# Bidirectional encoder in fp32: a doubled weight operand in DRAM, narrower reloads and a new instruction order

## The chip, the core and the metric

The kernel runs on one core of a Trainium2 chip, in one launch. A core has five instruction queues: TensorE (PE in the profile; the loading of its stationary operand is PEld), VectorE (DVE), ScalarE (ACT), GpSimd (POOL) and SyncE (SP). Data moves between DRAM and on-chip memory through 16 DMA engines, which are fed by SyncE's queue (q1 in the profile) and GpSimd's queue (q0). The metric is device time in microseconds (us), the median over the runs of one kernel; lower is better. The notebook-style names in the profile's rows, such as `wlo<-wraw,whi`, say which tile an instruction wrote and which it read.

## What is computed

Two layers (DEPTH = 2) over 256 tokens of width 4096, in fp32. Each layer is, cut from the reference:

```python
h = rmsnorm(x, norm_w[l])
proj = h @ w_in[l]                                   # 4096 x 11264
aq, ak, av, ag, rq, rk, rv, rg = jnp.split(proj, SPLIT_POINTS, axis=-1)
...
a_out = (jax.nn.silu(ag) * gqa_attention(aq, ak, av)).astype(x.dtype)
...
r = bidirectional_retention(rq, rk, rv, log_gf, log_gb).transpose(0, 2, 1, 3)
r = rmsnorm(r, ret_norm[l]).reshape(B, S, RET_WIDTH)
r_out = (jax.nn.silu(rg.astype(jnp.float32)) * r).astype(x.dtype)

x = x + jnp.concatenate([a_out, r_out], axis=-1) @ w_out[l]      # 4096 x 4096
```

Queries and keys of both branches go through an axial rotary embedding (those of attention through an RMSNorm per head as well); attention has 16 query heads over 4 key/value heads, retention 8 heads with a decay forward and one backward. A last RMSNorm follows the second layer. The two big products, `w_in` and `w_out` of each layer, are nearly all of the work.

## The kernel before, in words

**Stages and blocks.** There are four stages: the `w_in` product of layer 1 (11 blocks), its `w_out` product (4 blocks), and the same two for layer 2. A block makes 1024 columns of output for all 256 tokens, as two column halves of 512. It runs over all 4096 input features in 16 pairs of 128-feature slices (pair p holds slices 2p and 2p+1). The weights of one block and pair are a 256 x 1024 matrix, stored in DRAM as two pages of 128 partitions x 2 x 512 numbers (512 KB each).

**High and low parts.** TensorE multiplies fp32r numbers, which carry fewer bits than fp32. So each page is split: ScalarE casts it to a high part (`whi`, or `bhi` for a half page), VectorE subtracts that from the page and gets the low part (`wlo`, `blo`). The operand from x is split in the same way (`x8h`/`x8l`, `x7h`/`x7l`). One product is then three matmuls of 128 x 512: high by high, high by low, low by high (lines 1669 and 1679).

**Eights and sevens.** With two slices, two column halves and two token halves a pair needs 8 products, so 24 matmuls (tiles with an 8 in their name). For six of the 16 pairs (SEVENS) a Strassen-like scheme needs only 7 products, so 21 matmuls. That scheme takes sums of weight quarters. Page A of such a pair holds two diagonal quarters. The DRAM layout holds the other two as the "third" and one that is added to both halves of page A: ScalarE copies page A (`wraw`) to `wv`, and an accumulating DMA on GpSimd's queue (line 723) adds the off-diagonal quarter to both halves of `wv`, read from DRAM as a broadcast, twice the same 2 KB per partition. VectorE then makes two more sums, `wu`, from page A, `wv` and the third. So a product of a seven needs a chain: load of `wraw`, copy on ScalarE, DMA with add, cast on ScalarE, subtraction on VectorE. Its operands of x (`x7h`, `x7l`) need sums too (`xf`, in `split_pair`).

**What sets the order.** The program is written out by Python code that keeps a clock of its own (`Now`, `Clock`) and decides, matmul by matmul, what the other engines are told to do next: `tick` runs after every product, `Weights.proceed`, `low_parts`, `add_up` and `add` issue casts, subtractions, copies and adds, and `Weights.room` says whether there is room for a step of the other tasks. Such tasks are generators: rotary and transposes, attention, retention, residual and norms, and the making of the next stage's operands (`split_pair`). Every engine executes its own list in order. The constants of the planner (STEP_V, EARLY, LOW_AHEAD and so on) can differ by block: `assume(n)` loads BASE and the entry n of PLANS, with blocks counted from 0 to 29 over all stages. LATE goes into the gate of the attention tasks through `near(LATE)`.

**Order of the pairs.** In the first block of a stage the order of the pairs is that of `opening_order`: the eights in rising order, with the sevens inserted at the places of SPREAD (stage 1), SPREAD1, SPREAD2 and SPREAD3. A seven opens a group, and the pages of the eights in its group are put between its own pages.

**Buffers.** Raw pages (`wraw`) have 6 buffers, high parts 5 (RING), low parts 4 (LOWS), `wv` 2, `wu` 1. `Weights.empty` marks a raw page as read; the next load (line 523, SyncE) is told to go when the oldest page still held has been read, so pages are freed in order. A seven's page A is held until its sums `wu` are made.

**Handing on between stages.** Results of a block are turned (32 x 32 transposes on VectorE, `turned`), stored to DRAM by GpSimd (`store`, four DMAs) and fetched again as `full` pages by the next stage (line 916). The last two pages of a stage are not stored: ScalarE moves them on chip (`move`, tiles `ca` and `cb`), scales them by the norm's gains (`nw`) and splits them. Keys and values of attention lie in `kv_dram` as one page of four parts per group: high and low parts of the keys, high and low parts of the values. `attention_scores` uses the keys, `attention_rest` the values, and each fetches the whole page (lines 1315 and 1338). `retention_weights` fetches rk and rq of two heads with runs of 64 numbers (line 1352).

The functions that the diff touches follow.

Of the kernel before, what the change touches and what calls it, by code (L numbers as in the profile page):

```python
# [17 lines left out]
P = 128  # L18
# [9 lines left out]
NB = 512  # L28
# [3 lines left out]
MT = SEQ // P  # L32
NP = KT // 2
BLK = 32
ALL = slice(None)
PAGES = 13
RAWS = 6
SUMS = 2
# [5 lines left out]
STRICT = 4  # L44
RELIEF = 1.5
# [9 lines left out]
V_FIXED = 0.1  # L55
STT = 0.0
# [45 lines left out]
LATE = 25  # L102
# [9 lines left out]
    3: {'U_SLACK': 0.3, 'HOLD': 2, 'LOW_AHEAD': 1.0, 'STRICT': 4},  # L112
    7: {'V_FIXED': 0.14, 'RUSH': 1.0, 'ADD_SLACK': 0.3},
    8: {'SUM_SLACK': 1.0, 'ADD_SLACK': 0.3, 'TIGHT_A': 4, 'LOW_AHEAD': 5.0},
    17: {'EARLY': 1.8, 'V_FIXED': 0.14},
    22: {'TIGHT_B': 20, 'PASS': 0.1, 'STT': 0.0, 'RAW_SLACK': 3.0},
    23: {'RELIEF': 1.5, 'LOW_AHEAD': 5.0},
    24: {'LOW_AHEAD': 5.0},
    25: {'STRICT': 9, 'RUSH': 1.0},
# [216 lines left out]
def hybrid_encoder(  # L336
# [5 lines left out]
    w_out: bass.AP,  # L342
    norm_wT: bass.AP,
# [127 lines left out]
    class Seven:  # L471

        def __init__(self, w):
            self.third, self.added = w[1, :, 1, :], w[1, :, 0:1, :].to_broadcast([P, 2, NB])
            self.a = self.b = self.v = self.u = None
            self.a_at = self.b_at = self.v_at = self.u_at = 0.0

    class Weights:


        def __init__(self):
            self.pages, self.sevens = [], []
            for l in range(DEPTH):
                for w, n in ((w_in, N_IN), (w_out, N_OUT2)):
                    for b in range(n):
                        stage = 2 * l + (w is w_out)
                        start = (l, b) == (0, 0) and w is w_in
                        for g in GROUPS[stage] if b else FIRST_GROUPS[stage]:
                            for slot in slots_of(g, stage, start):
# [10 lines left out]
                                if one.seven:  # L500
                                    if one.kind == PAGE_A:
                                        self.sevens.append(Seven(w[l, b, one.pair]))
                                    one.own = self.sevens[-1]
# [6 lines left out]
            self.raws = [g for g in self.seq if not g.seven or g.kind == PAGE_A]  # L510
            self.placed, self.emptied, self.made = 0, 0, 0
# [655 lines left out]
    def rotary(v, L, kind, to):  # L1167
# [37 lines left out]
        turned(o, v)  # L1205
# [141 lines left out]
    def retention_weights(L, i):  # L1347

        raw = page([P, 2, 4 * MT, 2 * BLK], "rkq")
        for k in range(2):  # L1350
            src = rkq_dram[i // 2][k].rearrange("p (k n) -> p k n", k=4 * MT)
            nc.gpsimd.dma_start(raw[:, k], src[:, :, 2 * BLK * (i % 2) : 2 * BLK * (i % 2 + 1)])
# [3 lines left out]
        v = raw.rearrange("p k (a m) (i t) -> p k m i a t", m=MT, t=BLK)  # L1356
# [596 lines left out]
    for _ in range(RAWS + 1 - 2 * len(NATIVE)):  # L1953
        weights.load()
# [69 lines left out]
    "x", "xT", "w_in", "w_out", "norm_wT", "q_norm", "k_norm", "decay", "final_norm", "consts",  # L2024
# [45 lines left out]
```

## Time and profile before

| | |
|---|---|
| median of 3 runs | 2610.96 us (2609.42 to 2612.77) |
| profiled execution, device time | 2609.15 us |
| its span, first to last instruction | 2607.4 us |
| mean granted TensorE clock | 0.998 |
| DMA | 657.72 MB, mean 252 GB/s |
| queue of SyncE (q1) | 147040 packets, 472.99 MB, 51.5% of 16 engines |
| queue of GpSimd (q0) | 81696 packets, 181.44 MB, 31.4% of 16 engines |
| wraw loads | 776 of 512 KB |
| adds into wv | 180 of 512 KB |

How to read it: the time of a run is that of the profiled execution's kind, its span is 1.75 us shorter. A row of groups gives line, engine, operation, output and inputs, count, then busy us and the mean of one in ns, then idle time before it and what ended that. A row of stretches gives the stretch, its length, then busy us and instructions of PE, PEld, DVE, ACT and POOL, then the granted TensorE clock, the busy share of the DMA engines, and GB/s. A row of waits gives who waited for whom, us in total, times, longest. A timeline row gives start, us, engine, line, operation, tiles, count and, in brackets, idle time before it and its releaser. A row of DMA issues ends with the size in KB and the median us from issue to landing. A matmul of 128 x 512 is shown 0.39 us long while the next starts after 0.23 us, since matmuls overlap. On this kernel a change of under about 5 us can't be told from none.

### The profile page before, as it was taken

To read this page: it belongs to the slowest core of one execution; us is meant where nothing else is said; L and a number is where in the kernel's file an instruction comes from. 1 tells how busy PE (TensorE), PEld (TensorE's weight loads), DVE (VectorE), ACT (ScalarE), POOL (GpSimd) and SP (SyncE) were. 2 spreads that over 40 slices of the span, in tenths; PEclk is the share of its full clock that TensorE was granted. 3 is DMA by queue.
4 is the path that set the end of the run, shared out by engine and by line. 5 is a ranking of instruction groups with operands and counts; after the bars stand their busy time and mean duration, and the time that the engine had idled before them with its cause. 6 is when DMAs were issued, how large, how long until landed. Compare 5 with 4: busy or idle time off the path is not lost.

```text
span 2607.4 us, 34348 instructions
## 1 busy us (share of the span) xinstructions
PE 2585.2 (99%) x11560; PEld 2135.3 (82%) x11560; DVE 2213.8 (85%) x2702; ACT 1848.1 (71%) x2623; POOL 457.8 (18%) x548
## 2 busy tenths in 40 slices
PE   9999999999999999999999999999999999999998
PEld 6888888888888888888787888888888888888886
DVE  6898888888878898777888888889888798987777
ACT  7877776776666778656886667776676667786655
POOL 0112322221112101211112112221211111011110
PEclk9999999999999999999999999999999999999999
DMA  9988988988778777988888889888887797778886
GB/s 307 298 238 285 283 252 260 290 251 267 213 226 254 231 227 223 283 268 250 270 259 243 248 248 286 244 279 270 262 270 211 200 271 234 229 217 257 253 239 194
DMA packets 229634, 657.72 MB, mean 252 GB/s; under 512 B 24784, under 2 KB 31440, under 8 KB 229456
## 3 DMA queue, kind: packets, MB, share of 16 engines
q1 hardware_dynamic: 147040, 472.99, 51.5%
q0 software_dynamic: 81696, 181.44, 31.4%
q8 instruction: 90, 1.47, 0.2%
q10 hardware_dynamic: 720, 1.10, 0.1%
q14 instruction: 88, 0.72, 0.1%
HBM read 611.39 MB, written 44.04 MB: 251 GB/s over the span
## 4 chain that ended last, share of the span: by engine, by line
PE 90%; DMA 4%; DVE 2%; ACT 2%; issue 2%; POOL 0%; SPq 0%; DVEq 0%; POOLq 0%; ACTq 0%
PE M L1669 58%; PE M L1679 29%; PE M L1143 1%; PE M L1144 1%; PE M L1142 1%; DMA pT<-p_dram 1%; DMA wv<-in_w_in 1%; ACT whi L320 1%; DMA wv<-in_w_out 1%; DVE wlo L320 1%; DMA x_dram<-ca 1%; DMA full<-next_dram 0%; DMA wraw<-in_w_in 0%; DVE cb L320 0%; DMA wraw<-in_w_out 0%
## 5 line engine op out<-in xcount | busy, mean ns | idle before, releaser
L320 DVE TENSOR_TENSOR wlo<-wraw,whi 128x1024 fp32r<-128x1024 f32 (+1 forms) x774 | 935.3, 1215 | 159.3 <-issue 60.9
L320 ACT CAST whi<-wraw 128x1024 fp32r<-128x1024 f32 (+1 forms) x776 | 798.1, 1045 | 270.7 <-PE M L1669 259.5
L1669 PE MATMUL M<-whi,x8h 128*128 128x512 f32 x2368 | 923.5, 390 | 3.5 <-ACT x8h L320 2.9
L1669 PE MATMUL M<-whi,x8l 128*128 128x512 f32 x2368 | 922.5, 390 | 0.6 <-DVE x8l L320 0.6
L1679 PE MATMUL M<-wlo,x8h 128*128 128x512 f32 x2364 | 676.7, 389 | 1.4 <-DVE wlo L320 1.4
L1669 PEld LDWEIGHTS M<-whi,x8h 128*128 128x128 f32 x2368 | 445.1, 188 | 97.7 <-ACT x8h L320 3.7
L1669 PEld LDWEIGHTS M<-whi,x8l 128*128 128x128 f32 x2368 | 445.1, 188 | 93.4 <-DVE x8l L320 1.1
L1679 PEld LDWEIGHTS M<-wlo,x8h 128*128 128x128 f32 x2364 | 441.9, 188 | 93.4 <-DVE wlo L320 3.1
L1669 PE MATMUL M<-whi,x7h 128*128 128x512 f32 x1080 | 420.4, 389 | 0.0
L1669 PE MATMUL M<-whi,x7l 128*128 128x512 f32 x1080 | 420.3, 389 | 0.0
L723 POOL DMA_DIRECT2D wv<-in_w_in x132 | 162.2, 1230 | 1040.1 <-ACT wv L320 862.8
L1679 PE MATMUL M<-wlo,x7h 128*128 128x512 f32 x1080 | 334.1, 390 | 1.6 <-DVE wlo L320 1.5
L320 ACT CAST whi<-wv 128x1024 fp32r<-128x1024 f32 x180 | 189.2, 1051 | 133.0 <-DMA wv<-in_w_in 52.3
L320 DVE TENSOR_TENSOR wlo<-wu,whi 128x1024 fp32r<-128x1024 f32 x180 | 219.2, 1218 | 33.6 <-PE M L1679 19.9
L320 DVE TENSOR_TENSOR wlo<-wv,whi 128x1024 fp32r<-128x1024 f32 x180 | 219.5, 1220 | 32.0 <-PE M L1679 27.9
L320 ACT CAST whi<-wu 128x1024 fp32r<-128x1024 f32 x180 | 189.3, 1051 | 79.2 <-DVE wu L320 48.2
L320 ACT COPY wv<-wraw 128x1024 f32<-128x1024 f32 x180 | 188.9, 1049 | 78.9 <-DMA wraw<-in_w_in 39.8
L1679 PEld LDWEIGHTS M<-wlo,x7h 128*128 128x128 f32 x1080 | 202.1, 188 | 45.8 <-DVE wlo L320 4.1
L1669 PEld LDWEIGHTS M<-whi,x7h 128*128 128x128 f32 x1080 | 202.8, 188 | 42.3 <-ACT whi L320 0.3
L1669 PEld LDWEIGHTS M<-whi,x7l 128*128 128x128 f32 x1080 | 202.7, 188 | 41.9
L320 DVE TENSOR_TENSOR wu<-wraw,wv 128x512 f32<-128x512 f32 x180 | 123.4, 686 | 41.1 <-DMA wv<-in_w_in 24.7
L723 POOL DMA_DIRECT2D wv<-in_w_out x48 | 58.1, 1211 | 504.1 <-ACT wv L320 412.3
(249 smaller groups left out, 2381.5 us busy)
## 6 DMA issues: line engine op xcount, KB each, us to landing
wraw<-in_w_in SPq DMA_DIRECT2D x568, 512.0 KB, 5.1
wraw<-in_w_out SPq DMA_DIRECT2D x208, 512.0 KB, 5.1
wv<-in_w_in POOLq DMA_DIRECT2D x132, 512.0 KB, 8.1
third<-in_w_in SPq DMA_DIRECT2D x132, 256.0 KB, 5.6
wv<-in_w_out POOLq DMA_DIRECT2D x48, 512.0 KB, 8.8
third<-in_w_out SPq DMA_DIRECT2D x48, 256.0 KB, 5.3
full<-next_dram POOLq DMA_DIRECT2D x18, 512.0 KB, 9.6
kv<-kv_dram POOLq DMA_DIRECT2D x16, 512.0 KB, 8.6
```

What stands on the lines that cost most here:

```text
L320: return call(out, *args, **kwargs)
L723: self.adds.pop(0)[1]()
L1142: nc.tensor.matmul(out, a[0], b[0], start=start, stop=False)
L1143: nc.tensor.matmul(out, a[0], b[1], start=False, stop=False)
L1144: nc.tensor.matmul(out, a[1], b[0], start=False, stop=stop)
L1669: nc.tensor.matmul(acc[name], a[i], g.hi[h], start=m == first[name] and not i, stop=False)
L1679: nc.tensor.matmul(acc[name], a, g.lo[h], start=False, stop=m == final[name])
```

## The change

- **Doubled quarters.** The host writes for each of the pairs in EVER (the six sevens) the off-diagonal quarter twice side by side into new inputs `twice_in` and `twice_out`. The accumulating DMA into `wv` reads rows of 2 x 512 numbers (4 KB) there, instead of the same 512 numbers (2 KB) twice from the weights. The bytes that the DMA moves stay the same.
- **kv by halves.** `attention_scores` fetches parts 0 and 1 (keys) of the page, `attention_rest` parts 2 and 3 (values).
- **Rows by head.** rk and rq are turned by two transposes (one for each half of the tokens) into a layout in which the two heads that `retention_weights` reads have 128 numbers side by side instead of 64.
- **Free slots.** The six raw buffers are six tiles of their own. A page that is read frees its slot at once, and the next load takes the slot that has been free longest. A loop that would move the first page of sevens ahead by A_EARLY places is added, with A_EARLY = 0.
- **Orders.** LATE goes from 25 to 35. The entries of PLANS are replaced. SPREAD, SPREAD1 and SPREAD3 are changed, SPREAD2 is not.

The diff, without the lines that only pass the new inputs on:

```diff
-LATE = 25
+LATE = 35
...
-    22: {'TIGHT_B': 20, 'PASS': 0.1, 'STT': 0.0, 'RAW_SLACK': 3.0},
...
+    14: {'STRICT': 9, 'TIGHT_A': 0},
+    15: {'S_FIXED': 0.16, 'LONG': 2, 'EARLY': 1.8, 'PASS': 0.3, 'PE_REST': 2.0, 'NEAR': 30},
...
-SPREAD = (4, 5, 7, 10, 12, 14)
-SPREAD1 = (4, 7, 8, 10, 12, 13)
+SPREAD = (3, 5, 8, 11, 12, 13)
+SPREAD1 = (4, 7, 8, 10, 12, 14)
 SPREAD2 = (2, 3, 6, 7, 10, 13)
-SPREAD3 = (4, 7, 8, 9, 10, 13)
+SPREAD3 = (6, 7, 9, 11, 12, 14)
...
-        def __init__(self, w):
-            self.third, self.added = w[1, :, 1, :], w[1, :, 0:1, :].to_broadcast([P, 2, NB])
+        def __init__(self, w, twice):
+            self.third, self.added = w[1, :, 1, :], twice
...
+            for i, g in enumerate(self.raws):
+                if g.seven and i > RAWS + A_EARLY:
+                    self.raws.insert(i - A_EARLY, self.raws.pop(i))
+            self.slots = [f"wraw{_i}" for _i in range(RAWS)]
...
-                g.raw = t(wp, [P, 2, NB], "wraw", RAWS)
+                g.slot = self.slots.pop(0)
+                g.raw = t(wp, [P, 2, NB], g.slot, 1)
...
-            g.empty = True
-            while self.emptied < len(self.raws) and self.raws[self.emptied].empty:
-                self.emptied += 1
-                self.load()
+            self.slots.append(g.slot)
+            self.load()
...
+    def turned_by_head(src, room):
+
+        for m in range(MT):
+            ve.transpose(
+                room.rearrange("p (b i m t) -> p m b i t", b=4, i=4, m=MT)[:, m],
+                src[:, m, :].rearrange("p (i b e) -> p b i e", i=4, e=BLK),
+            )
...
-        turned(o, v)
+        (turned if kind in ("aq", "ak") else turned_by_head)(o, v)
...
-        nc.gpsimd.dma_start(kv, kv_dram[g])
+        nc.gpsimd.dma_start(kv[:, 0:2, :], kv_dram[g][:, 0:2, :])
...
-        nc.gpsimd.dma_start(kv, kv_dram[g])
+        nc.gpsimd.dma_start(kv[:, 2:4, :], kv_dram[g][:, 2:4, :])
...
-        raw = page([P, 2, 4 * MT, 2 * BLK], "rkq")
+        raw = page([P, 2, 4, 2 * MT * BLK], "rkq")
         for k in range(2):
-            src = rkq_dram[i // 2][k].rearrange("p (k n) -> p k n", k=4 * MT)
-            nc.gpsimd.dma_start(raw[:, k], src[:, :, 2 * BLK * (i % 2) : 2 * BLK * (i % 2 + 1)])
+            src = rkq_dram[i // 2][k].rearrange("p (a f) -> p a f", a=4)
+            nc.gpsimd.dma_start(raw[:, k], src[:, :, 2 * MT * BLK * (i % 2) : 2 * MT * BLK * (i % 2 + 1)])
...
+    def twice(o):
+
+        d = np.empty(o.shape[:2] + (len(EVER), P, 2, NB), o.dtype)
+        for i, p in enumerate(EVER):
+            for h in range(2):
+                d[:, :, i, :, h] = o[:, :, p, 1, :, 0]
+        return d
```

Apart from the added transposes and three PSUM copies (`out<-M`) that ScalarE now makes, every engine executes the same instructions as before; the order of TensorE's 11566 rows differs in 289, those of VectorE and ScalarE in about half, mostly by neighbours that have changed places.

More of the change, by code (lines that the diff above doesn't have):

```diff
@@ L37 @@
 RAWS = 6
+A_EARLY = 0
 SUMS = 2
@@ L483, in __init__ @@
             for l in range(DEPTH):
-                for w, n in ((w_in, N_IN), (w_out, N_OUT2)):
+                for w, twice, n in ((w_in, twice_in, N_IN), (w_out, twice_out, N_OUT2)):
                     for b in range(n):
@@ L501, in __init__ @@
                                     if one.kind == PAGE_A:
-                                        self.sevens.append(Seven(w[l, b, one.pair]))
+                                        self.sevens.append(Seven(w[l, b, one.pair], twice[l, b, EVER.index(one.pair)]))
                                     one.own = self.sevens[-1]
@@ L1952, in hybrid_encoder @@
         weights.load()
-    for _ in range(RAWS + 1 - 2 * len(NATIVE)):
+    while weights.slots:
         weights.load()
@@ L2045, in tiled @@
         return o
+    def twice(o):
[4 more added lines that the diff above has]
+        return d
+    w_in = tiled(a["w_in"], [[FIRST[k] + NB * i for k, i in b] for b in BLOCKS])
+    w_out = tiled(a["w_out"], [[2 * NB * n, 2 * NB * n + NB] for n in range(N_OUT2)])
     given = {
@@ L2049 @@
         "xT": np.ascontiguousarray(x.T.reshape(NCH, KG, P, SEQ).transpose(0, 2, 1, 3)).reshape(NCH, P, KG * SEQ),
-        "w_in": tiled(a["w_in"], [[FIRST[k] + NB * i for k, i in b] for b in BLOCKS]),
-        "w_out": tiled(a["w_out"], [[2 * NB * n, 2 * NB * n + NB] for n in range(N_OUT2)]),
+        "w_in": w_in,
+        "w_out": w_out,
+        "twice_in": twice(w_in),
+        "twice_out": twice(w_out),
         "norm_wT": np.concatenate([a["norm_w"].reshape(-1, P), a["ret_norm"].reshape(-1, P)]).T,
```

19 lines of the change are left out of this document (10 added, 9 removed).

## The prediction

> **What bounds the kernel now.** I read the page's engine table first, then busy time by stretch, then TensorE's waits, then the timeline around the largest of them. The page:
>
> ```profile
> span 2607.4 us, 34348 instructions
> PE 2585.2 (99%) x11560; PEld 2135.3 (82%) x11560; DVE 2213.8 (85%) x2702; ACT 1848.1 (71%) x2623; POOL 457.8 (18%) x548
> ```
>
> TensorE is idle for 2607.4 - 2585.2 = 22.2 us. Its matmuls stay the same in kind and number, so a new order or faster transfers can win only what TensorE loses to waits. Busy time by stretch (first busy column is PE) shows where:
>
> ```profile
> 0.00:20.00 20.00, 17.98 (x53) 8.91 (x53) 7.73 (x14) 12.27 (x21) 0.49 (x5) 1.00 0.90 347
> 20.00:70.00 50.00, 48.06 (x205) 37.64 (x205) 42.17 (x62) 43.49 (x70) 5.92 (x5) 1.00 0.93 288
> 600.00:610.00 10.00, 9.78 (x43) 7.75 (x42) 6.50 (x7) 5.47 (x6) 0.00 (x0) 1.00 1.03 365
> 1240.00:1345.00 105.00, 103.24 (x448) 83.15 (x447) 90.76 (x123) 86.48 (x137) 17.40 (x19) 1.00 0.88 263
> 1371.00:1378.00 7.00, 4.63 (x15) 3.32 (x14) 4.72 (x8) 6.24 (x14) 0.00 (x0) 0.76 0.64 218
> 1895.00:1905.00 10.00, 8.90 (x39) 6.74 (x38) 5.33 (x6) 4.23 (x5) 0.00 (x0) 1.00 0.94 322
> 2570.00:2590.00 20.00, 19.01 (x82) 15.05 (x81) 19.53 (x30) 8.35 (x15) 0.00 (x0) 1.00 0.20 57
> 2590.00:2607.40 17.40, 5.62 (x25) 4.32 (x23) 7.10 (x17) 5.35 (x10) 1.13 (x2) 0.76 0.64 242
> ```
>
> The differences (2.02, 1.94, 0.22, 1.76, 2.37, 1.10, 0.99, 11.78) add up to 22.18 us: eight places hold all the idle time. The first and the last, 13.8 us, are the first loads and the final normalisation with its stores, which the change leaves alone. Six places in the middle hold 8.38 us. TensorE waits there for the engines that make its operands:
>
> ```profile
> PE M L1679 <- DVE wlo L320: 2.9, 6, 0.6
> PE M L1669 <- ACT x8h L320: 2.9, 2, 2.4
> PE M L1143 <- DVE pTl L320: 1.0, 2, 0.8
> PE M L1669 <- DVE x8l L320: 0.6, 1, 0.6
> ```
>
> A wait costs more than its idle time. An undisturbed stretch of the timeline, then a small wait, then the largest:
>
> ```profile
> 1002.24 1.07 PE L1679 MATMUL M<-wlo,x8h 128*128 128x512 f32 x4
> 1003.15 0.39 PE L1669 MATMUL M<-whi,x7h 128*128 128x512 f32 x1
> ...
> 1265.86 0.39 PE L1669 MATMUL M<-whi,x8l 128*128 128x512 f32 x1
> 1266.81 1.19 PE L1679 MATMUL M<-wlo,x8h 128*128 128x512 f32 x4 [0.56 <-DVE wlo L320]
> 1267.84 0.40 PE L1669 MATMUL M<-whi,x7h 128*128 128x512 f32 x1
> ...
> 1370.96 0.61 PE L1679 MATMUL M<-wlo,x7h 128*128 128x512 f32 x2
> 1373.94 0.80 PE L1669 MATMUL M<-whi,x8h 128*128 128x512 f32 x1 [2.37 <-ACT x8h L320]
> ...
> 1377.06 0.39 PE L1669 MATMUL M<-whi,x8l 128*128 128x512 f32 x1
> ```
>
> Undisturbed, four matmuls start in 0.91 us, 0.227 each. At 1265.86 five starts take 1.98 instead of 1.14: 0.84 lost for 0.56 of idle, 0.28 on top. At 1370.96 the next pair should start at 1371.41 and starts at 1373.94 (2.53 lost); the seven starts after it take 3.12 instead of 1.59, because the granted clock falls to a mean of 0.76 in that window (1.53 lost). That wait costs 4.06 us.
>
> The Trainium skill (TensorE: Matmul & The Clock Gate, "What's actually happening") says the clock halves after an idle window of about 3.4 us; by it this 2.37 us wait would cost 2.53 and its removal 1.5 us less than I count below. The trace shows the slow matmuls after the shorter idle, so the trace decides.
>
> The six places, at 0.28 on top of each wait: 20 to 70 us 1.94 + 4 x 0.28 = 3.1; 606 us 0.5; 1240 to 1345 us 1.76 + 4 x 0.28 = 2.9; 1371 us 4.1; 1900 us 1.7; 2578 us 1.5. Together 13.8 us, or 0.53%: the most that this change can win.
>
> **The change, part by part.**
>
> *Orders at the start of layer 2 (1371 us).* ScalarE's order, where pair 14's operand (x8h) is made from the late page cb. Before:
>
> ```order
> L320 CAST whi_12353<-wraw_12233 128x1024
> L320 CAST whi_12376<-wv_12240 128x1024
> L320 CAST bhi_12378<-third_12238 128x512
> L320 CAST whi_12391<-wraw_12285 128x1024
> L320 ACTIVATE cb_11636<-cb_11636,nw_97 128x8x32 x2
> L320 CAST x8h_12403<-cb_11636 128x256 x2
> L320 COPY ca_12408<-M1_11872 128x512
> ```
>
> The same place in the changed kernel (names differ by a running number; 12381, 12406, 12408 and 12421 are 12353, 12376, 12378 and 12391 of before):
>
> ```order
> L321 ACTIVATE cb_11650<-cb_11650,nw_97 128x8x32 x2
> L321 CAST x8h_12361<-cb_11650 128x256 x2
> L321 ACTIVATE cb_11650<-cb_11650,nw_97 128x8x32 x2
> L321 CAST x8h_12376<-cb_11650 128x256 x2
> L321 CAST whi_12381<-wraw1_12245 128x1024
> L321 CAST whi_12406<-wv_12279 128x1024
> L321 CAST bhi_12408<-third_12277 128x512
> L321 CAST whi_12421<-wraw2_12286 128x1024
> ```
>
> Four weight casts that stood ahead of x8h now stand behind it, and pair 15's operand comes directly after. TensorE's own order here is the same row for row.
>
> ```profile
> L320 ACT CAST whi<-wv 128x1024 fp32r<-128x1024 f32 x180 | 189.2, 1051 | 133.0 <-DMA wv<-in_w_in 52.3 <-PE M L1669 41.1 <-DMA wv<-in_w_out 33.9
> L320 ACT CAST bhi<-third 128x512 fp32r<-128x512 f32 x180 | 111.1, 617 | 10.9 <-PE M L1669 10.0 <-DMA third<-in_w_in 0.8
> ```
>
> x8h comes up to 3 x 1.05 + 0.62 = 3.8 us sooner, more than the 2.4 us wait, and then the clock has no reason to fall: -4.1. Next late are the moved casts: TensorE needs the first of them 12 matmuls (2.72 us) after x8h. ScalarE makes pair 15's operand (two scalings, two casts) and one cast meanwhile; that leaves little. And ScalarE is nearly full before this place (last window below, 34.35 of 37 us): if TensorE arrives 2 us sooner because earlier waits went, part of the wait returns. I keep -3.0; ends 0 and -4.1.
>
> *Doubled quarters: `wv` by 4 KB rows.* The 180 accumulating adds move the same bytes in half as many packets. The trace has accumulating DMAs of both shapes: into ca from in_x (2 KB runs) and from x_dram (4 KB rows). Issue to landing, and then GpSimd's time to issue (ns, min/median/max):
>
> ```profile
> wraw<-in_w_in SPq DMA_DIRECT2D x568, 512.0 KB, 5.1
> wv<-in_w_in POOLq DMA_DIRECT2D x132, 512.0 KB, 8.1
> ...
> kv<-kv_dram POOLq DMA_DIRECT2D x16, 512.0 KB, 8.6
> ...
> ca<-in_x POOLq DMA_DIRECT2D x4, 512.0 KB, 11.1
> ...
> ca<-x_dram POOLq DMA_DIRECT2D x3, 512.0 KB, 8.1
> ```
>
> ```profile
> L1785 POOL DMA_DIRECT2D ca<-in_x x4: 1197/1209/1219, 1051.5 to 1305.3; - x4
> ...
> L1785 POOL DMA_DIRECT2D ca<-x_dram x3: 887/900/900, 2347.4 to 2513.3; - x3
> ```
>
> So GpSimd saves 0.3 us an add, and the landing goes from 11.1 to 8.1, a ratio of 0.73, in busier and quieter places of the run. On 8.1 us that would be 2.2 us; the bounds are 0.3 (issue alone) and 2.2 us. What the queues did in one window of each (2 KB, then 4 KB; packets, MB, share):
>
> ```profile
> q0 software_dynamic: 813, 1.57, 63.1%
> q1 hardware_dynamic: 664, 2.27, 44.4%
> ```
>
> ```profile
> q0 software_dynamic: 280, 1.05, 66.8%
> q1 hardware_dynamic: 305, 1.14, 34.9%
> ```
>
> The windows are 13.7 us (from 1053.8) and 9.1 us (from 2349.5). An MB on q0 cost 13.7 x 16 x 0.631 / 1.57 = 88 us of engine time by 2 KB and 9.1 x 16 x 0.668 / 1.05 = 93 by 4 KB: the larger packet saves no transfer time. But the adds' queue takes a larger turn: q1, which brings raw pages, moved 166 GB/s beside the first and 125 beside the second. I take 1.5 us sooner per add, between the bounds.
>
> The Trainium skill (DMA: Bandwidth & Descriptors, "Queues, rings and completion order") says an engine switches between queues only at a packet's end. That speaks against the change, since raw pages then wait longer; the two windows agree, 44.4% against 34.9%.
>
> Where does `wv` decide? In 1240 to 1345 us. Landing there (window 1240 to 1266), and two windows of that stretch:
>
> ```profile
> wraw<-in_w_out SPq DMA_DIRECT2D x7, 512.0 KB, 9.1
> wv<-in_w_out POOLq DMA_DIRECT2D x3, 512.0 KB, 12.1
> ```
>
> ```profile
> 1265.00:1305.00 40.00, 38.30 (x165) 30.12 (x163) 39.24 (x61) 35.94 (x60) 3.94 (x4) 1.00 0.75 229
> 1335.00:1372.00 37.00, 36.51 (x159) 29.27 (x157) 31.22 (x40) 34.35 (x56) 3.73 (x4) 1.00 0.74 239
> ```
>
> VectorE works without a gap from 1265 to 1305 (39.24 of 40 us), late because the adds before landed after 12.1 us. GpSimd's order at this place is unchanged except for the adds' shape. Two adds 1.5 us sooner give VectorE up to 3 us: most of 2.9 goes. I take -2.0; ends 0 and -2.9.
>
> *Opening of layer 1 (20 to 70 us).* SPREAD puts the first seven-product pair fourth instead of fifth. ScalarE, before and then after:
>
> ```order
> L320 CAST x7h_186<-xf_188 128x640
> L320 CAST whi_209<-wraw_146 128x1024
> L320 COPY wv_217<-wraw_150 128x1024
> L320 COPY wv_221<-wraw_152 128x1024
> L320 CAST whi_235<-wraw_148 128x1024
> ```
>
> ```order
> L321 COPY wv_204<-wraw2_146 128x1024
> L321 CAST x7h_186<-xf_188 128x640
> L321 CAST whi_213<-wraw2_146 128x1024
> L321 COPY wv_221<-wraw5_152 128x1024
> L321 CAST whi_231<-wraw3_148 128x1024
> ```
>
> The first add starts from the third raw page instead of the fifth, but TensorE also reaches its products one eight-product pair, 24 x 0.227 = 5.4 us, sooner; the pages of pair 4 now stand between its sums, where none stood. A new order in a stretch whose DMA engines are 93% busy can lose as well: -1.0, ends +3 and -3.1. The other openings that SPREAD1 and SPREAD3 touch show no wait now: 0, at worst +1 together.
>
> *kv by halves, rows by head.* Half of the 16 kv transfers' bytes go (8.6 us each on GpSimd's queue), ahead of the pT loads on which 606 and 1900 us wait: -0.8 of 2.2; ends 0 and -2.2. The rq/rk transposes become two instructions of half size: 8 more on VectorE, at most the 0.69 us of a 512-column operation each,
>
> ```profile
> L320 DVE TENSOR_TENSOR wu<-wraw,wv 128x512 f32<-128x512 f32 x180 | 123.4, 686 | 41.1 <-DMA wv<-in_w_in 24.7 <-DMA wv<-in_w_out 16.4
> ```
>
> 5.5 us spread over VectorE's 393 idle us: 0, up to +0.7 if one meets a wait. *Free slots.* A_EARLY is 0, so its loop moves nothing, and the loads' order on SyncE is that of before in all but 36 of 1016 rows: 0. *2578 us:* the same order, VectorE full (19.53 of 20): 0. *Elsewhere* (LATE, plans): attention and retention products move by a few matmuls; I add +0.8 for one or two new waits of the present size; ends 0 and +4.
>
> Sum: -3.0 - 2.0 - 1.0 - 0.8 + 0.8 = -6.0 us. The profiled execution took 2609.15 us (span 2607.4 and 1.75 around it) and gives 2603.15; the median of the three runs, 2610.96, gives 2605.0. No change can be told from one of under about 0.2% (5.2 us).
>
> **Rivals.** *The waits move on:* TensorE, sooner at 1300, meets the same full ScalarE at 1371, and new orders cost what they save: -1, 2610.0. For it: both engines are full there. Against it: the casts moved are worth more than the wait. *Nearly every wait goes:* -11, 2600.0; against it, 2578 us is untouched. *Slower: raw pages starve.* Beside 4 KB adds q1 slows by 166/125 = 1.33, so 9.1 us becomes 12.1. Six slots cover 6 x 2.72 = 16.3 us of matmuls; while a seven's page holds one for its add, five cover 13.6, less about 2.3 for high and low parts: 11.3. Past that point a load is 0.8 us late; 7 loads in each of three full stretches (20 to 70 us counts twice) give 17 us, less 6.0: +11, 2622.0. Against it: loads land after 5.1 us in the median, and the adds are in flight for a shorter time.
>
> **Chances.** The forecast's case 0.60 (2601 to 2609, 0.70 of it past the 0.2%), waits moving on 0.22, nearly all gone 0.07, raw pages starving 0.11. Faster: 0.42 + 0.07 = 0.49; slower 0.11; same 0.40. The range 2599 to 2612 leaves out the slower case and the edge of the best one.
>
> **What would show it.** Right: no wait on x8h near 1370 and a granted clock of 1.00 there; `wv` landing in about 6.6 us; VectorE with gaps from 1265 to 1305. Wrong: ScalarE or VectorE waiting for wraw more than before, wraw landing well over 5.1 us, or new waits over 1 us in the openings.

## The result and the profile after

The changed kernel takes 2599.24 us (median of 5 runs, 2597.27 to 2599.46); the kernel before took 2610.96 us beside it (5 runs, 2608.96 to 2614.19). The changed kernel is 11.7 us faster by the medians. The ratio is 0.9953, 95% interval 0.9938 to 0.9967, which is 0.47% or 12.3 us: about twice the forecast of 6.0. The profiled execution took 2599.34 us, with a span 9.8 us shorter than before. Its page:

```profile
span 2597.6 us, 34368 instructions
PE 2581.8 (99%) x11560; PEld 2135.2 (82%) x11560; DVE 2215.3 (85%) x2710; ACT 1853.6 (71%) x2626; POOL 398.6 (15%) x548
```

TensorE is idle for 15.8 us instead of 22.2, and is 3.4 us less "busy" with the same 11560 matmuls: that fits fewer matmuls at a lowered clock or right behind a wait, which the busy time counts as longer. The stretches that answer to those of before (all lie some us earlier now; first busy column is PE, the third DVE, the fourth ACT, and the figure after POOL the granted clock):

```profile
20.00:70.00 50.00, 50.00 (x221) 41.22 (x220) 46.24 (x70) 46.55 (x75) 4.34 (x5) 1.00 0.94 301
600.00:610.00 10.00, 10.00 (x46) 8.21 (x45) 7.75 (x11) 4.11 (x4) 1.33 (x2) 1.00 0.91 316
1240.00:1345.00 105.00, 104.25 (x453) 84.03 (x452) 92.57 (x130) 91.26 (x147) 14.90 (x19) 1.00 0.87 258
1368.00:1375.00 7.00, 7.00 (x32) 5.63 (x31) 6.96 (x9) 7.00 (x10) 0.00 (x0) 1.00 0.76 239
1378.00:1385.00 7.00, 6.20 (x27) 4.79 (x26) 6.86 (x10) 3.24 (x4) 2.48 (x3) 1.00 0.89 222
1890.00:1905.00 15.00, 15.00 (x68) 12.35 (x67) 12.92 (x17) 7.97 (x11) 1.09 (x2) 1.00 0.92 271
2565.00:2585.00 20.00, 19.39 (x85) 15.56 (x85) 17.75 (x31) 8.26 (x16) 0.57 (x1) 1.00 0.12 45
```

Three places have no idle time left (20 to 70, 606, 1900 us), and the wait at 1371 us is gone with its slow clock. What remains in the middle is 0.75 + 0.80 + 0.61 = 2.16 us of idle, in five waits; two of 0.2 us each (on `ca` and `whi`) are left out here:

```profile
PE M L1693 <- DVE wlo L321: 0.8, 2, 0.6
PE M L1683 <- DVE cb L321: 0.8, 1, 0.8
```

The wait on `cb` at 1381 us is new. Counted as in the prediction, with 0.28 us on top of each wait, the middle places cost 2.16 + 5 x 0.28 = 3.6 us now against 13.8: 10.2 us less, which is the span's 9.8 within half a us. The medians differ by 1.9 us more than the spans, nearly all of it because the profiled execution of the kernel before was 1.8 us faster than its median (2609.15 against 2610.96).

The landing of the transfers (last figure, median us) and the two groups that wait for the adds:

```profile
wraw<-in_w_in SPq DMA_DIRECT2D x568, 512.0 KB, 5.2
wv<-in_twice_in POOLq DMA_DIRECT2D x132, 512.0 KB, 7.5
wv<-in_twice_out POOLq DMA_DIRECT2D x48, 512.0 KB, 8.1
pT<-p_dram POOLq DMA_DIRECT2D x16, 512.0 KB, 9.9
kv<-kv_dram POOLq DMA_DIRECT2D x16, 256.0 KB, 7.6
```

```profile
L321 ACT CAST whi<-wv 128x1024 fp32r<-128x1024 f32 x180 | 189.0, 1050 | 91.5 <-PE M L1683 51.9 <-DMA wv<-in_twice_in 18.5 <-DMA wv<-in_twice_out 13.9
L321 DVE TENSOR_TENSOR wu<-wraw,wv 128x512 f32<-128x512 f32 x180 | 123.1, 684 | 8.7 <-DMA wv<-in_twice_in 6.3 <-DMA wv<-in_twice_out 2.3
```

An add lands only 0.6 us sooner in the median (7.5 instead of 8.1), yet VectorE's idle time before `wu` fell from 41.1 to 8.7 us and ScalarE's before the cast of `wv` from 133.0 to 91.5. That pair of rows is the first sign that a median landing doesn't tell what an add is worth, though the new orders have a part in it too. `pT` and `kv` land sooner in the median as well; the experiments on them show below why this isn't what freed 606 and 1900 us.

### The profile page after: what moved, and what is told of

Its sections match the earlier page's. It is cut to its first block, busy times and chain, and to the rows that moved or that the text cites. A ratio compares the mean times of both kernels' runs of the same rounds, so it can differ in the third digit from the quotient of the medians.

```text
span 2597.6 us, 34368 instructions
## 1 busy us (share of the span) xinstructions
PE 2581.8 (99%) x11560; PEld 2135.2 (82%) x11560; DVE 2215.3 (85%) x2710; ACT 1853.6 (71%) x2626; POOL 398.6 (15%) x548
## 4 chain that ended last, share of the span: by engine, by line
PE 94%; DMA 2%; DVE 2%; ACT 1%; issue 1%; SPq 0%; DVEq 0%; POOLq 0%; POOL 0%; ACTq 0%
PE M L1683 60%; PE M L1693 30%; PE M L1158 1%; PE M L1157 1%; PE M L1156 1%; DMA ca<-in_x 1%; DVE wlo L321 1%; ACT whi L321 1%; DMA third<-in_w_out 0%; PE M L1677 0%; DMA wraw<-in_w_out 0%; DVE cb L321 0%; DMA whole<-in_w_in 0%; ACT ca L321 0%; DVE ca L321 0%
## 5 line engine op out<-in xcount | busy, mean ns | idle before, releaser
L729 POOL DMA_DIRECT2D wv<-in_twice_in x132 | 118.5, 898 | 1068.6 <-ACT wv L321 923.8
L321 ACT CAST whi<-wv 128x1024 fp32r<-128x1024 f32 x180 | 189.0, 1050 | 91.5 <-PE M L1683 51.9
L321 DVE TENSOR_TENSOR wu<-wu,third 128x512 f32<-128x512 f32 x180 | 124.6, 692 | 7.0 <-DMA third<-in_w_in 0.8
```

Of the source, the lines that this page charges most:

```text
L321: return call(out, *args, **kwargs)
L729: self.adds.pop(0)[1]()
```

## The experiments

Each group of four ran on one chip beside runs of the kernel before (medians there 2609.14, 2610.22, 2609.90 and 2610.68 us). Differences between kernels of different groups are taken from the ratios, times 2610 us. An interval is some 2 to 4 us to either side, so a difference between two of these kernels is seldom certain by the times alone. The clearest are E6 and E7 beside E5: on one chip, no execution of either is as fast as the slowest of E5.

| | kernel | median, us | ratio to before, 95% interval |
|---|---|---|---|
| E1 | tables alone on the kernel before | 2605.69 | 0.9990 (0.9982 to 0.9999) |
| E2 | changed, old tables | 2610.37 | 1.0004 (0.9995 to 1.0013) |
| E3 | changed, adds as before | 2601.68 | 0.9968 (0.9956 to 0.9981) |
| E4 | changed, kv and rows as before | 2599.26 | 0.9963 (0.9950 to 0.9975) |
| E5 | changed, once more | 2598.95 | 0.9957 (0.9945 to 0.9970) |
| E6 | changed, old SPREAD | 2602.18 | 0.9969 (0.9958 to 0.9981) |
| E7 | changed, no plans 14 and 15 | 2601.85 | 0.9966 (0.9954 to 0.9979) |
| E8 | changed, old slot rule | 2599.30 | 0.9959 (0.9945 to 0.9973) |
| E9 | doubled quarters alone on before | 2605.05 | 0.9983 (0.9974 to 0.9992) |
| E10 | E2 with the old slot rule | 2605.15 | 0.9983 (0.9975 to 0.9992) |
| E11 | changed, old SPREAD3 | 2604.61 | 0.9985 (0.9976 to 0.9993) |
| E12 | changed, no plans 22 and 24 | 2600.59 | 0.9964 (0.9952 to 0.9977) |
| E13 | E9 with two copies in 2 KB rows | 2608.91 | 0.9993 (0.9984 to 1.0002) |
| E14 | changed, two copies in 2 KB rows | 2602.82 | 0.9970 (0.9959 to 0.9980) |
| E15 | kv and rows alone on before | 2606.96 | 0.9989 (0.9980 to 0.9997) |
| E16 | tables and doubled quarters alone | 2599.76 | 0.9963 (0.9950 to 0.9977) |

**E1 and E2: tables or transfers?** E1 puts the new numbers into the kernel before; E2 puts the old ones into the changed kernel:

```diff
-LATE = 25
+LATE = 35
 PLANS = ...        (all entries, E1 new, E2 old)
-SPREAD = (4, 5, 7, 10, 12, 14)
+SPREAD = (3, 5, 8, 11, 12, 13)
-SPREAD1 = (4, 7, 8, 10, 12, 13)
+SPREAD1 = (4, 7, 8, 10, 12, 14)
-SPREAD3 = (4, 7, 8, 9, 10, 13)
+SPREAD3 = (6, 7, 9, 11, 12, 14)
```

> The kernel before with the new numbers alone (LATE, PLANS, SPREAD, SPREAD1, SPREAD3); adds, kv, retention rows and slots as before. Theory 'orders' (the tables removed the waits of the two openings, 3.1 and 4.1 us): 2610.96 - 7 = about 2604, no wait on x8h at 1371 us, no idle from 20 to 70 us, the pT waits at 606 and 1900 us still there. Rival 'transfers' (quicker adds and shorter queue removed them): -2 or less, about 2609, waits in the openings still there. Rival 'both are needed' (the tables were chosen for the new transfers): 2611 or slower, new waits elsewhere.

> The changed kernel with the old numbers (LATE, PLANS, SPREAD, SPREAD1, SPREAD3): the new transfers and slots alone. Theory 'orders': -3 to -4 from the kernel before, about 2607, pT waits at 606 and 1900 us gone, the x8h wait at 1371 us and its clock of 0.76 still there. Rival 'transfers': -8 or more, 2603 or faster, x8h wait smaller than 1 us.

Measured: -2.6 us for E1 and +1.0 for E2, against -11.2 to -12.3 for both. None of the theories had that; "both are needed" comes nearest. E1 has no idle time from 20 to 70 us, but it keeps `pTl` at 1897 us and waits at new places, above all on `cb` twice:

```profile
PE M L1669 <- DVE cb L320: 1.6, 2, 0.8
...
PE M L1143 <- DVE pTl L320: 0.8, 1, 0.8
```

E2 loses the waits at 606 and 1900 us, but keeps the one at 1370 us and has two new ones near 2308 and 2330 us. ScalarE and TensorE at the second:

```profile
2328.05 1.05 ACT L321 CAST whi<-wv 128x1024 fp32r<-128x1024 f32 x1 [1.46 <-PE M L1693]
2329.01 0.61 ACT L321 CAST bhi<-third 128x512 fp32r<-128x512 f32 x1
2329.53 1.04 ACT L321 CAST whi<-wraw 128x1024 fp32r<-128x1024 f32 x1
2330.47 0.70 ACT L321 CAST x8h<-ca 128x256 fp32r<-128x256 f32 x2
...
2331.23 0.50 PE L1683 MATMUL M<-whi,x8h 128*128 128x512 f32 x1 [1.93 <-ACT x8h L321]
```

It is the picture of 1371 us in the kernel before: three weight casts, the first of which waits for a buffer that TensorE holds, stand ahead of the operand. In the kernel before, `x8h` stands ahead of them here.

**E10: what moved the casts in E2.** The same with `Weights.empty` freeing pages in the order of their loads again:

```diff
-            self.slots.append(g.slot)
-            self.load()
+            g.empty = True
+            while self.emptied < len(self.raws) and self.raws[self.emptied].empty:
+                self.slots.append(self.raws[self.emptied].slot)
+                self.emptied += 1
+                self.load()
```

> The changed kernel with the old tables (as in e2_orders_old) and also the old rule for slots. Theory 'the free slots under the old tables moved ScalarE's casts ahead of the operand x8h near 2328 us': the waits of e2 near 2308 and 2329 us (about 5 us with the slower clock behind them) are gone, 2605, waits at 606 and 1900 us gone too. Rival 'the transfers themselves make those waits': they stay, 2610.

2605.15 us, as expected by the first theory: 5.5 us faster than E2 by the ratios, no wait near 2308 or 2330 us. TensorE's and SyncE's order in E10 is that of the kernel before row for row, and ScalarE's differs from it only in two casts that have each moved past two neighbours; in E2 it differs in many places. The free slots cost those 5.5 us through the planner: loads that it issues elsewhere move its clock, and with that its choices hundreds of us later. No run has the free slots under the order of E10, so a cost of the slots themselves isn't shown or ruled out.

**E5 and E8: the free slots under the new tables.** E8 makes the edit of E10 in the changed kernel; E5 is the changed kernel itself on the same chip.

> The changed kernel once more, beside the next three and on their chip: 0.995 to 0.996 of the kernel before, and executions within 3 us of each other, whatever the theory. It is what the next three are held against.

> The changed kernel with raw pages that take slots again only in the order of their loads. Theory 'free slots are worth nothing' (six slots cover a load of 5 us): within 0.5 us of the changed kernel. Rival 'the free slots bring raw pages sooner, so the tables could be packed closer': ScalarE and VectorE wait for wraw longer, new waits of TensorE, 2 us slower or more.

E5 gave 2598.95 and E8 2599.30: no difference that can be told. E5's profile has no wait on `cb` at 1381 us at all, so the one new wait comes and goes between executions. LATE has no effect here at all: with LATE = 25 the changed kernel's order is the same on every engine.

**E6: SPREAD.**

```diff
-SPREAD = (3, 5, 8, 11, 12, 13)
+SPREAD = (4, 5, 7, 10, 12, 14)
```

> The changed kernel with SPREAD alone put back to (4, 5, 7, 10, 12, 14): the old opening of layer 1 with the new transfers. Theory 'the table removed the waits': the idle of 20 to 70 us comes back at 1.7 us or more, about 3 us slower than the changed kernel. Rival 'the adds' earlier landing removed them': less than 0.5 us of idle there, the same time.

```profile
20.00:70.00 50.00, 47.90 (x207) 38.13 (x206) 42.56 (x62) 43.26 (x70) 3.95 (x5) 1.00 0.90 286
```

2602.18 us, 3.2 more than E5, and 2.10 us of idle against 1.94 before: the table, not the quicker adds, removed the waits of layer 1's opening, and removed all of them. E1, which has the table without the quicker adds, has no idle time there either.

**E7: the plans of blocks 14 and 15.**

```diff
-    14: {'STRICT': 9, 'TIGHT_A': 0},
-    15: {'S_FIXED': 0.16, 'LONG': 2, 'EARLY': 1.8, 'PASS': 0.3, 'PE_REST': 2.0, 'NEAR': 30},
```

> The changed kernel without the two plans of blocks 14 and 15, which puts ScalarE's four weight casts ahead of pair 14's operand again, as in the kernel before. Theory 'the place of the casts sets the wait': the x8h wait of about 2.4 us and a granted clock below 0.8 are back near 1365 us, the 0.96 us wait on cb at 1381 us is gone, 3 us slower than the changed kernel. Rival 'TensorE was late for other reasons, or arrives later now': a wait of under 1 us there, clock 1.00, within 1 us of the changed kernel.

The place in E7's timeline, then its stretch:

```profile
1364.02 1.04 ACT L319 CAST whi<-wv 128x1024 fp32r<-128x1024 f32 x1
...
1364.96 0.61 ACT L319 CAST bhi<-third 128x512 fp32r<-128x512 f32 x1
...
1365.48 1.04 ACT L319 CAST whi<-wraw 128x1024 fp32r<-128x1024 f32 x1
...
1367.24 0.69 ACT L319 CAST x8h<-cb 128x256 fp32r<-128x256 f32 x2
...
1367.98 0.50 PE L1681 MATMUL M<-whi,x8h 128*128 128x512 f32 x1 [2.41 <-ACT x8h L319]
```

```profile
1365.00:1372.00 7.00, 4.59 (x15) 3.13 (x14) 4.76 (x8) 6.81 (x14) 0.00 (x0) 0.83 0.65 229
```

2601.85 us, 2.9 more than E5. The wait of 2.41 us on `x8h` is back behind the casts, with a clock of 0.83; the casts' place is the cause. In exchange there is no wait at 1381 us (7.00 of 7 us busy from 1378 to 1385).

**E11 and E12: the tables that I had counted at nothing.** Only SPREAD3 put back (E11); only the entries 22 and 24 of PLANS left out (E12).

```diff
-SPREAD3 = (6, 7, 9, 11, 12, 14)
+SPREAD3 = (4, 7, 8, 9, 10, 13)
```

```diff
-    22: {'PASS': 0.3, 'U_SLACK': 1.0, 'AT_ONCE': 1},
-    24: {'V_FIXED': 0.12, 'TIGHT_B': 20, 'TIGHT_A': 2},
```

> The changed kernel with SPREAD3 alone put back to (4, 7, 8, 9, 10, 13). My estimate in the prediction was 0 for this table, since the opening of layer 2's second matrix showed no wait before. Theory 'it only keeps the new code from a wait': ScalarE now has six casts between the scaling and the operand x8h near 2325 us, a wait there of 1 to 4 us, 2 to 5 us slower than the changed kernel. Rival 'no matter': the same time.

> The changed kernel without the plans of blocks 22 and 24. Pair 14's operand x8h near 2328 us is then made ten rows later on ScalarE. Theory 'the late plans keep a wait away there': a wait on x8h of 2 us or more near 2328 us with a lower clock, 2 to 4 us slower than the changed kernel. Rival 'the operand is in time all the same': within 0.5 us.

E11 costs 7.3 us by the ratios, 5.7 by the medians, at another place than I had read from the order: not `x8h` near 2325 us, but the first seven of the last stage, where ScalarE waits for a raw page before it can copy it to `wv`, and the cast of the third comes late:

```profile
2271.86 1.05 ACT L321 COPY wv<-wraw 128x1024 f32<-128x1024 f32 x1 [1.83 <-DMA wraw<-in_w_out]
...
2272.82 1.04 ACT L321 CAST whi<-wv 128x1024 fp32r<-128x1024 f32 x1
...
2273.76 0.61 ACT L321 CAST bhi<-third 128x512 fp32r<-128x512 f32 x1
...
2274.39 0.47 PE L1683 MATMUL M<-whi,x7h 128*128 128x512 f32 x1 [2.27 <-ACT bhi L321]
```

So this table wins nothing against the kernel before (no wait there) and still is worth several us: it keeps the rest of the change from new waits (E11 has another 1.16 us of idle in two waits on `wlo` from 2290 to 2310 us). E12 has no wait near 2328 us; its 1.8 us lie within the interval.

**E3 and E9: the doubled quarters, taken out and alone.** E3 puts the broadcast back into the changed kernel; E9 brings only the new source into the kernel before, with every engine's order unchanged.

```diff
-            self.third, self.added = w[1, :, 1, :], twice
+            self.third, self.added = w[1, :, 1, :], w[1, :, 0:1, :].to_broadcast([P, 2, NB])
```

> The changed kernel with the adds read as before (one quarter broadcast, 2 KB rows), every order the same. Theory 'orders': 1 us slower than the changed kernel, about 2600, since wv landed only 0.6 to 0.7 us sooner with 4 KB rows. Rival 'transfers': 4 us slower or more, 2603, with VectorE and ScalarE waiting for wv again before the waits of TensorE. Rival 'larger packets hold the raw pages up': faster than the changed kernel by up to 1 us.

> The kernel before with the doubled quarters alone: every engine's order row for row that of before, only the adds read 4 KB rows. Theory 'a small help': the quarters were worth 2.4 us in the changed kernel, so 2 to 3 us here, about 2607.5, the x8h wait of 2.4 us at 1371 us still there. Rival 'worth something only under the new tables': within 1 us of the kernel before. Rival '4 KB packets hold the raw pages up': slower by 1 us or more.

E3 is 2.9 us slower than the changed kernel, between its two theories and not beyond the intervals; E9 is 4.4 us faster than the kernel before, more than either expectation. Where E9's gain lies, first the crowded stretch and the pT place at 1900 us, then the landing from 1240 to 1266 us:

```profile
1265.00:1305.00 40.00, 40.00 (x177) 32.74 (x176) 39.21 (x63) 33.49 (x56) 5.56 (x6) 1.00 0.74 230
1365.00:1375.00 10.00, 7.43 (x26) 5.48 (x25) 7.63 (x11) 8.88 (x18) 0.00 (x0) 0.83 0.53 195
1895.00:1905.00 10.00, 9.84 (x43) 7.79 (x42) 7.50 (x10) 5.33 (x9) 0.89 (x1) 1.00 0.94 324
```

```profile
wraw<-in_w_out SPq DMA_DIRECT2D x7, 512.0 KB, 7.7
wv<-in_twice_out POOLq DMA_DIRECT2D x3, 512.0 KB, 8.4
```

In that stretch an add lands after 8.4 us instead of 12.1, and TensorE's 1.70 us of idle from 1265 to 1305 are gone. And at 1900 us 0.16 us of idle are left of 1.10, 606 us is free of any: `pT` comes over the same GpSimd queue and lands after 11.0 us instead of 11.7 over the whole run. Layer 1's opening (1.81 us of idle) and 1371 us are as before.

**E13 and E14: the size of the rows, or reading twice?** The quarters are stored as two copies apart from each other, so that an add reads 2 KB rows again, each once (the diff is cut):

```diff
-        d = np.empty(o.shape[:2] + (len(EVER), P, 2, NB), o.dtype)
+        d = np.empty(o.shape[:2] + (len(EVER), 2, P, NB), o.dtype)
...
-                d[:, :, i, :, h] = o[:, :, p, 1, :, 0]
+                d[:, :, i, h] = o[:, :, p, 1, :, 0]
```

> The kernel before with the doubled quarters stored as two separate copies, so that an add still reads 2 KB rows, but no row twice. Every order is that of before. Theory 'the rows' size does it': as the kernel before, about 2610, GpSimd 1.2 us for an issue, wv landing after 8 us. Rival 'reading the same rows twice was the cost': as e9_twice_alone, about 2605.

> The changed kernel with the same two separate copies (2 KB rows). Theory 'the rows' size': as e3_no_twice, 2 to 3 us slower than the changed kernel, about 2601.5. Rival 'reading twice was the cost': as the changed kernel, 2599.

E13, the same stretch and landing, then VectorE's group in E13 and in E9:

```profile
1265.00:1305.00 40.00, 38.60 (x166) 30.32 (x165) 39.25 (x60) 35.12 (x59) 4.74 (x5) 1.00 0.73 230
```

```profile
wv<-in_twice_out POOLq DMA_DIRECT2D x3, 512.0 KB, 11.5
```

```profile
L321 DVE TENSOR_TENSOR wu<-wraw,wv 128x512 f32<-128x512 f32 x180 | 123.3, 685 | 43.0 <-DMA wv<-in_twice_in 25.1 <-DMA wv<-in_twice_out 17.9
L321 DVE TENSOR_TENSOR wu<-wraw,wv 128x512 f32<-128x512 f32 x180 | 123.1, 684 | 15.8 <-DMA wv<-in_twice_in 9.9 <-DMA wv<-in_twice_out 5.9
```

The landing (11.5), the idle time (1.40 us) and VectorE's waiting (43.0) are close to the kernel before (12.1, 1.70 and 41.1) and far from E9 (8.4, none and 15.8). The times lie near the kernel before and near E3 (ratios 0.9993 and 0.9970). The times alone would leave it open, since the intervals of E9 and E13 overlap; with these rows it is the size of the rows that decides how long VectorE waits for an add. E13 leaves only 0.59 us of idle at 606 and 1900 us, though, with `pT` after 11.1 us, so how much of E9's gain at those two places comes from the size isn't shown.

Two more pairs differ by the doubled quarters alone: E10 has E15's order on every engine, and E16 has E1's. VectorE's idle time before `wu` falls in each pair as well, from 45.5 to 18.5 us and from 28.8 to 16.2. By the ratios the quarters are worth 1.6 us in the first and 7.0 in the second, where the two intervals don't touch. So their price depends on the orders around them. Under the new tables it can't be found in the crowded stretch: from 1240 to 1345 us TensorE is idle for 1.07, 0.91 and 0.45 us with 2 KB rows (E1, E3, E14) and for 0.75, 0.98 and 1.25 with 4 KB rows (changed kernel, E5, E16). The profiles of E3 and E14 are of each one's fastest execution (2599.07 and 2599.70 us) and have hardly more idle time in the middle than the changed kernel's (2.36 and 2.30 us against 2.16), so where their other executions lose some 3 us stays open.

**E15, E4 and E16: kv by halves, rows by head.** E15 makes these edits alone in the kernel before, E4 takes them out of the changed kernel, E16 is the kernel before with the new tables and the doubled quarters only. The main lines of E4's edit:

```diff
-        nc.gpsimd.dma_start(kv[:, 0:2, :], kv_dram[g][:, 0:2, :])
+        nc.gpsimd.dma_start(kv, kv_dram[g])
...
-        (turned if kind in ("aq", "ak") else turned_by_head)(o, v)
+        turned(o, v)
```

> The kernel before with kv by halves and rows by head alone. Theory 'they shorten the queue ahead of pT': the waits at 606 and 1900 us (2.2 us with what follows them) go, 2 us faster than before. Rival 'moved products and the eight added transposes cost what that saves': within 1 us.

> The changed kernel with kv fetched whole twice and the retention rows in their old layout; adds, slots and tables as changed (the planner moves some later products, since the two half transposes are one again). Theory 'the queue ahead of pT': pT lands about 1.8 us later, the waits at 606 and 1900 us come back, 2 to 3 us slower than the changed kernel, about 2602. Rival 'the tables moved the products away from the late pT': within 0.5 us of the changed kernel, about 2599, no wait on pT.

> The kernel before with the new tables and the doubled quarters, and nothing else (kv whole, old retention rows, old slots). Theory 'tables and adds are the change': 2599 to 2600, at least 9.5 us of the 11 us. Rival 'every part is needed by the tables': 2602 or slower.

E15 is 2.9 us faster than the kernel before, and both places are free:

```profile
600.00:610.00 10.00, 10.00 (x46) 8.20 (x45) 6.98 (x8) 6.77 (x8) 1.29 (x2) 1.00 0.99 372
1895.00:1905.00 10.00, 10.00 (x46) 8.21 (x44) 6.98 (x7) 6.72 (x8) 1.29 (x2) 1.00 1.00 374
```

But the theory has the wrong reason. GpSimd's issues at the second place, in the kernel before and in E15, each followed by the landing of that `pT` load (window 1870 to 1888):

```profile
1884.06 2.28 POOL L1104 DMA_DIRECT2D rq_dram<-cb  x4 [3.38 <-DVE cb L320]
1886.33 0.58 POOL L1338 DMA_DIRECT2D kv<-kv_dram  x1
...
1887.43 0.58 POOL L1109 DMA_DIRECT2D pT<-p_dram  x1
...
pT<-p_dram POOLq DMA_DIRECT2D x1, 512.0 KB, 12.2
```

```profile
1882.56 1.07 POOL L1355 DMA_DIRECT2D kv<-kv_dram  x1
...
1883.67 1.05 POOL L1126 DMA_DIRECT2D pT<-p_dram  x1
1887.43 2.22 POOL L1121 DMA_DIRECT2D rq_dram<-cb  x4 [2.71 <-DVE cb L321]
...
pT<-p_dram POOLq DMA_DIRECT2D x1, 512.0 KB, 13.7
```

From its issue `pT` takes no less time than before (13.7 us against 12.2; at 606 us 12.4 against 11.2), with half the bytes of kv ahead of it. What changed is GpSimd's order: the kv, `sgT` and `pT` loads stand ahead of the four stores of rq, which wait for VectorE's `cb`, and `pT` is issued 6.1 us sooner after the last add (1.85 instead of 7.97 us; at 606 us 5.8 sooner). Apart from VectorE's half transposes and a few neighbours that have changed places there and on ScalarE, these two places are all that differs in order between E15 and the kernel before. Written out with one edit at a time, the program gets this order from the rows by head alone, while the halves alone leave every order as before; neither was run.

At 1900 us the other kernels agree: the loads stand behind the stores in the kernel before, E1, E4, E9, E13 and E16, which all have idle time there (0.16 to 1.10 us), and ahead of them in all others, which have none. At 606 us the new tables put them ahead too (E1, E4 and E16, no idle time). Taken out of the changed kernel (E4) the two edits cost 1.6 us by the ratios and nothing by the medians, within the interval either way, though `pTl` waits 0.8 us again in its profile. E16 is 9.7 us faster than the kernel before, of the 11.2 of E5.

## Why the prediction was wrong

The direction was right, and the ceiling of 13.8 us held. The sum was too small by about half, and the rival with a chance of 0.07, that nearly every wait goes, is what happened. By the sum's own terms, from the two profiles, counted alike (0.28 us on top of a wait):

| term | forecast | measured in the profile | by experiment |
|---|---|---|---|
| layer 2's opening | -3.0 | -4.1 + 1.1 (new wait at 1381 us) | 2.9 (E7) |
| 1240 to 1345 us, adds | -2.0 | 0.75 + 3 x 0.28 against 2.9: -1.3 | old orders (E9): 0.60 + 0.28, so -2.0; new orders: 0.91 us idle without the quarters (E3), 0.75 and 0.98 with them |
| layer 1's opening | -1.0 | -3.1 | 3.2 (E6) |
| 606 and 1900 us | -0.8 | -2.2 | E15 takes all of it, E9 most |
| 2578 us | 0 | 0.61 + 0.28 against 1.5: -0.6 | none made |
| new waits elsewhere | +0.8 | 0 (the one at 1381 us is in the first row) | |
| sum | -6.0 | -10.2 | |

**The step that failed** is the discount, which mis-sized three terms. Where an edit reached a wait, I took a part of it for fear of contention: a third of layer 1's opening (-1.0, measured -3.1), a third of the pT places (-0.8, measured -2.2), and 0.8 us more for new waits (measured 0). These make 4.3 us; the rest, 0.6 us better at 2578 us and 0.7 worse from 1240 to 1345, nearly cancels. In layer 1's opening I feared that TensorE would reach its products 5.4 us sooner and starve; the stretch now runs without a gap at a DMA share of 0.94, and E6 shows that the order of the pairs alone decides that. A wait is not a load that a change lightens in part: it goes whole once its operand comes earlier by more than the wait, as `x8h` did. What may come is another wait behind it: E1, with the new tables and the old transfers, keeps 1.24 us of idle in layer 2's opening (0.8 on `cb`, 0.4 on `x8h`).

**The pT places** were also wrong in mechanism. I counted bytes in GpSimd's queue, and read its order only from 1240 to 1266 us. The runs show that the order of its issues took these waits away: the `pT` load is issued about 6 us sooner, ahead of the stores, and takes as long as before to land (E15). That the bytes of kv are worth anything is not shown.

**Layer 2's opening** was right in mechanism, and in size with some luck. The casts' place makes the wait (E7). The -3.0 fits the profiled execution and E7's 2.9 us; in E5's profile the new wait is missing, and whether the slow clock adds its 1.5 us differs from run to run, as shown below. ScalarE is indeed full where TensorE arrives sooner (7.00 of 7), and the next late thing is the one new wait, but on VectorE's `cb`, not on the moved casts.

**The adds.** For the kernel before the place was right, 1240 to 1345 us, and so was its -2.0 (E9). In the changed kernel it is not shown: the new orders bring that stretch to the same idle time with the old adds (E1, E3), so the -1.3 there is mostly theirs. The step "1.5 us sooner per add" was off both ways: 0.6 us in the median, 3.7 us in the crowded stretch (E9). I also gave 606 and 1900 us to kv alone: E9's 4.4 us are about the 2.0 of that stretch and most of the 2.2 of these places. VectorE "with gaps from 1265 to 1305" was the wrong sign to look for: it is as full as before (39.21 of 40 in E9), only in time. The rival in which raw pages starve did not come: wraw of `w_in` lands after 5.2 us instead of 5.1, that of `w_out` after 5.4 instead of 5.1, and in the crowded stretch sooner (7.7 for 9.1 in E9).

**Slots and tables.** Free slots: 0 was right for the change as made (E8), but my reason, that nearly all loads keep their order, was not: under the old tables the same edit cost 5.5 us through the planner's order (E2, E10). SPREAD3 at 0 was right as a difference to the kernel before and wrong as a price: without it the change loses 5.7 to 7.3 us (E11). These parts do not add up one by one: the tables are worth 2.6 us with the old transfers (E1), and the rest of the change nothing that can be told with the old tables (E2). That each set of numbers fits one set of load and step times is the likely reason, not a shown one.

What stays open: why SPREAD3's old order has the raw page late at 2271 us (no run separates its page order from its casts), whether E12's 1.8 us are real, where the changed kernel gains from the doubled quarters (E3, E14), and what kv by halves is worth by itself.

## What to carry to other kernels

Where an engine is 99% busy, list its waits by place, find for each what stands ahead of the late operand, and let an edit that brings the operand earlier by more than the wait take the whole wait off the sum; keep doubt for the chance, not for the size. Then ask what is late next. Price a transfer by its landing in the stretch where someone waits for it, not by its median, and look at when it is issued and behind what, not only at its bytes. Where a planner writes the order, an edit of its clock is a change of order everywhere after it: compare the engines' lists before pricing the edit, and choose its tables again with it.

## What the runs showed of the hardware

**Row size of accumulating transfers.** GpSimd's queue (packets, MB, share of the engines' time) in E9 and in E13:

```profile
q0 software_dynamic: 58656, 181.44, 30.7%
```

```profile
q0 software_dynamic: 81696, 181.44, 31.7%
```

The same bytes in fewer, larger packets take nearly the same engine time, but the adds land sooner: 0.5 to 0.6 us in the median of those of `w_in` (7.5 in E9, 8.0 in E13, 8.1 before), and 3.1 to 3.7 us from 1240 to 1266 us (8.4 against 11.5 and 12.1, three adds in one execution of each). The Trainium skill (DMA: Bandwidth & Descriptors, "Queues, rings and completion order") has an engine change queues only at a packet's end; by it the adds gain a larger turn, and the landing agrees. The loss that I expected from it for the raw pages is there, but small: those of `w_out` land after 5.2 to 5.5 us in the median in every kernel with 4 KB rows but E8 (5.1), and after 5.0 to 5.1 in every one with 2 KB rows.

**The clock after a wait.** The length of the wait doesn't decide whether the clock falls. After 1.93 us of idle in E2 it fell; after 2.27 us in E11 and 2.5 us in E13 it did not (the granted clock stands behind POOL; windows around the wait of E2, E11 and E13):

```profile
2329.00:2336.00 7.00, 5.07 (x15) 3.56 (x14) 4.77 (x8) 6.06 (x12) 0.00 (x0) 0.76 0.51 170
```

```profile
2271.00:2278.00 7.00, 4.73 (x27) 3.83 (x27) 6.22 (x12) 6.10 (x10) 0.91 (x1) 1.00 0.81 209
```

```profile
1370.00:1377.00 7.00, 4.48 (x19) 3.33 (x19) 5.46 (x9) 6.46 (x13) 0.00 (x0) 1.00 0.68 266
```

E9 and E13 have the same order on every engine, and in E9 the clock fell to a mean of 0.83 after a wait of 2.57 us at this place. So the 1.53 us that I put on top of the wait at 1371 us needn't come with it. The Trainium skill (TensorE: Matmul & The Clock Gate, "What's actually happening") describes a free-running window of about 3.4 us; that the place in such a window decides fits these rows but is not shown by them, and that a whole window must be idle doesn't fit.
